# A hybrid SSD and GLA layer on one core: the order of the first block's start, and the step in which gates and the first y are made in blocks two to four

## The chip, the cores and the metric

The kernel runs on one core of one Trainium2 chip. The core has TensorE (PE, matmuls), VectorE (DVE), ScalarE (ACT), GpSimd (POOL) and SyncE (SP), which issues most transfers. The metric is the device time of one execution in microseconds, the median of three runs. Here it is 2259.13 us, with runs from 2258.09 to 2264.15.

## The reference

One decoder layer over 16 meta tokens and 2048 real tokens of width 1024, in float32. What is computed, cut to its core:

```python
u = rmsnorm(hres, norm_w)
proj = jnp.einsum('bld,dn->bln', u, w_in)          # one projection for all branches
z, xbc, dt_raw, q, k, v, g_gla, a_lr, merge_g = split_cols(proj, IN_WIDTHS)
# SSD branch: depthwise causal conv + silu on xbc, then a chunked scan with
# dt = softplus(dt_raw + dt_bias), decay exp(cumsum(dt * a)); y * silu(z), group rmsnorm
# GLA branch: log_a = log_sigmoid(a_lr @ gate_w2 + gate_b) / 16, chunked scan of q, k, v
# with cumsum(log_a); rmsnorm, * silu(g_gla)
branch_proj = jnp.einsum('blnc,ncd->blnd', branches, w_branch)
merged = jnp.sum(sigmoid(merge_g) * branch_proj, axis=2)
out = rmsnorm(hres + merged @ w_out, final_norm_w)[:, N_META:]
```

## The kernel before, in words

The 2048 tokens are cut into four blocks of 512 (the first also holds the 16 meta tokens). For each block all input projections but the merge gates are made, and the two scans are run; results go to DRAM. After the four blocks the merge gates, the two branch projections and the output projection follow as a chain of large matrix products, which the change does not touch.

**Matmuls in three parts.** Every operand is split into a rounded high part (ScalarE, Copy to fp32r) and a low remainder (a subtraction on VectorE for activations, on POOL for weights). `accum` (L207 to L211) issues three matmuls: high by high (L209), high by low (L210), low by high (L211). In block one the weights come raw from DRAM and are split by `load_w` (L163): the rounding is L171, the remainder L172. The split halves are stored (`save`, L201 to L205) and the later blocks read them back. There are 3 buffers for raw weights and 4 for split ones.

**The start.** `load_u` (L265) makes the normalised input u of a block. It squares and sums the rows, raises the mean to -1/2 on POOL (L279), spreads that over the partitions by matmuls with the identity (L317, L321), and then for each of eight tiles kt: load, normalise on VectorE (L333; in block one once for the 16 meta tokens and once for 512), round on ScalarE (L336), store, remainder on VectorE (L338). Behind it four small constants are halved on VectorE (L356 to L362).

**Pieces and steps.** In a block `enter` walks through a chain of pieces of TensorE work: generators such as `proj_zm` (the first z group, the step sizes dt and the gates' low-rank input), `proj_conv` (four tiles of one convolution group, one piece each), `proj_z` (block one) or `proj_z12` (other blocks), then the GLA projections. After each piece `step` advances every running generator by one part: `dt_chain`, `gates`, `ssd_scan`, `gla_scan`, `fetch_u`, `beside_unit`. Numbering pieces from n = 0, the pieces of a block are in sixes; with n = 6 * i the SSD scan of unit i - 1 begins.

- `gates` turns the low-rank input by TensorE (L460), evicts it, and for two pairs of heads multiplies by gw2 (L473), evicts it twice (L475 on VectorE, L476 on ScalarE), takes Exp (L478) and Ln (L479), then per head subtracts (L483) and runs sums along the chunks (L485). It begins at n = 6 in block one and at n = 8 in the others (L986).
- `ssd_scan` has a part for fetching, then `before(c)` and `after(c)` for four chunks: transposes (L637), their evictions (L640 to L646), the decay matrix on ScalarE (L650, L652) and its product with the scores on VectorE (L653); matmuls (L662, L663, L665), and their evictions (L668 to L675). A part scales by the root mean square (L703), and the last turns y by eight transposes (L708), evicts it on ScalarE (L710) and stores it (L711). The first unit begins at n = 6, so its y is turned at n = 13, the step of the last piece of `proj_z12`, whose banks are evicted by L494 and L495.

**What sets the order.** TensorE and SP issue in program order (a manual schedule, L1010). The order of VectorE, ScalarE and POOL is picked by a planner, which plays the program through with modelled times. `tc.issue_after(ins)` puts the instructions of a block behind `ins` on its engine; it adds an order, not a wait between engines. Banks of PSUM come from three pools: `pj` (3), `pt` (3) and `pc` (2).

Of the kernel before, what the change touches and what calls it, by code (L numbers as in the profile page):

```python
# [15 lines left out]
P = 128  # L16
# [21 lines left out]
T_SSD = 0  # L38
# [5 lines left out]
def trunk_kernel(ctx: ExitStack, tc: tile.TileContext, xm, xmt, w_feat, w_tok, w_v3, w_zm, w_br, w_o,  # L44
# [116 lines left out]
    kept, unsaved = {}, []  # L161

    def load_w(key, src):  # L163
        n = src.shape[-1]
        hl = mk(wpool, [P, 2, 512], F32R, "whl", bufs=4)[:, :, :n]
        if key in kept:
            nc.sync.dma_start(hl.bitcast(F32), kept[key])
        else:
            save(2)
            raw = raws.pop(key) if key in raws else load_raw(src)  # L170
            nc.scalar.activation(hl[:, 0], raw, AF.Copy)  # L171
            nc.gpsimd.tensor_tensor(hl[:, 1], raw, hl[:, 0].bitcast(F32), op=ALU.subtract)  # L172
# [20 lines left out]

    raws = {}

# [69 lines left out]
    def load_u(b):  # L265
# [10 lines left out]
        def rstd_rows(ss, n):  # L276
            r = mk(sm, [P, 1], F32, "rs1")
            nc.vector.tensor_scalar(r[:n], ss[:n], 1.0 / D, EPS, op0=ALU.mult, op1=ALU.add)
            nc.gpsimd.tensor_tensor(r[:n], r[:n], mhalf[:n, 0:1], op=ALU.pow)  # L279
            return r  # L280

# [27 lines left out]
        if m0:  # L309
            rs.append(rm_s)  # L310
            nc.sync.dma_start(cst[:, :2], cf32[:, :2])
# [12 lines left out]
        else:  # L324
            rbc = mk(spool, [P, 3 + META + BLK], F32, "cin")[:, :BLK]
            nc.scalar.activation(rbc, rb, AF.Copy)
            rbs = [(rbc, 0, BLK)]
            yield
        for kt in range(KT):
            xk = (mk(wk, [P, META + BLK], F32, "act", bufs=NACT) if m0 else mk(spool, [P, META + BLK], F32, "acc"))[:, :tt]  # L330
            nc.sync.dma_start(xk, xmt[:, kt, row0:row0 + tt])
            for ps, a, n in rbs:
                nc.vector.scalar_tensor_tensor(xk[:, a:a + n], xk[:, a:a + n], norm_w[:, kt:kt + 1], ps[:, :n],  # L333
                                               op0=ALU.mult, op1=ALU.mult)
            u.append(u_tile(b)[:, :, :tt])
            nc.scalar.activation(u[kt][:, 0], xk, AF.Copy)  # L336
            nc.scalar.dma_start(u_left[b][kt], xk[:, m0:])
            nc.vector.tensor_tensor(u[kt][:, 1], xk, u[kt][:, 0].bitcast(F32), op=ALU.subtract)  # L338
            yield
        return u  # L340

    next_u = {}

# [10 lines left out]

    hcw = const.tile([P, 16, 4], F32, name="hcw")
    nc.vector.tensor_scalar(hcw, conv_w, 0.5, None, op0=ALU.mult)  # L356
    hcb = const.tile([P, 16], F32, name="hcb")
# [3 lines left out]
    hgw = const.tile([P, 2], F32, name="hgw")  # L361
    nc.vector.tensor_scalar(hgw, gla_w, 0.5, None, op0=ALU.mult)  # L362
    nega = const.tile([P, NH], F32, name="nega")
    nc.scalar.activation(nega, hv[:, 1], AF.Exp)
# [39 lines left out]
    def dt_chain(o, psd):  # L404
# [12 lines left out]
        e = wde[:, :nck]  # L417
        nc.scalar.activation(e, x, AF.Abs)
        nc.scalar.activation(e, e, AF.Exp, scale=-1.0)
# [33 lines left out]
    def gates(o):  # L453
# [12 lines left out]
        for h2 in range(0, GH, 2):  # L466
# [14 lines left out]
            for h in (h2, h2 + 1):  # L481
                with tc.issue_after(convd[-1].ins) if m0 else nullcontext():
                    nc.vector.tensor_tensor(gmt[:, h % 2, :tt], gmt[:, h % 2, :tt], g_all[:, h, :tt], op=ALU.subtract)  # L483
                    for a, n in chunks:
                        nc.vector.tensor_tensor_scan(g_all[:, h, a:a + n], ones[:, :n], gmt[:, h % 2, a:a + n], 0.0,  # L485
                                                     op0=ALU.mult, op1=ALU.add)
                yield

# [11 lines left out]
    def proj_zm(o):  # L500
# [3 lines left out]
        yield from proj_tok("zm", w_zm, o.u, o.starts + [0] * o.ci0, list(enumerate(pss)), 288, 1, 256)  # L504
        begin(dt_chain(o, pss[NCH:] + pss[:NCH]))
        for c, ps in enumerate(pss[:NCH]):
            gate_z(zs[:, c], ps[:, :256])
        yield
# [82 lines left out]
    def ssd_scan(o, g):  # L591
# [37 lines left out]
        def before(c):  # L629
# [18 lines left out]
            with behind() if o.b == 0 else nullcontext():  # L648
# [3 lines left out]
                nc.scalar.activation(dm, dm, AF.Exp, scale=-1.0)  # L652
            nc.vector.tensor_tensor(dm, dm, scm[:, c].unsqueeze(1).to_broadcast([P, 4, P]), op=ALU.mult)  # L653
            held[c] = xdt, xw, bt, dm
# [47 lines left out]
        for c in range(NCH):  # L702
            nc.scalar.activation(yt[:, c], yt[:, c], AF.Identity, scale=r[:, c:c + 1])  # L703
        yield
        for j in range(2):
            ps = bank(pt, "pt")
# [246 lines left out]

    running, begun, lastly = [], [], []

    def begin(gen):
        begun.append(gen)

    def step():
        running.extend(begun)  # L960
        begun.clear()
        for gen in list(running) if len(running) < 2 or not lastly else list(running)[::-1]:
            if next(gen, running) is running:
                running.remove(gen)

    def beside_unit(key):
# [5 lines left out]
    def enter(pieces, o):  # L972
        b = o.b
        total = 6 * (SG + GH) + (b == nblk - 1)
        for n in range(total + 1):
            i, r = divmod(n, 6)
            if r == 0:
# [513 lines left out]
```

## Time and profile before

| | |
|---|---|
| median of 3 runs | 2259.13 us (2258.09 to 2264.15) |
| profiled execution | 2259.97 us, span 2257.6 us |
| mean granted TensorE clock | 0.996 |
| PE busy | 2217.3 us (98%) |
| DVE / ACT / POOL busy | 1575.8 / 1188.0 / 687.7 us |
| DRAM traffic | 517.94 MB in transfers, mean 229 GB/s |

A timeline row reads: start, duration in us, engine, source line, operation, output <- inputs, shapes, count; in square brackets the idle time before it and what ended that. A row of waits reads: engine, tile and line, what it waited for, us in total, times, the longest. A row of windows gives, for one stretch, the busy time of each engine with its instructions in brackets, then the granted TensorE clock (1.00 is full), the mean busy share of the 16 DMA engines, and GB/s. "x6" in a row means that six neighbours of one form were merged.

### The profile page before, as it was taken

The numbers are of one execution on the slowest core, as the hardware profiler recorded it, in microseconds if no ns is written. First come the engines' busy times: TensorE is split into PE (matmuls) and PEld (weight loads), VectorE is DVE, ScalarE is ACT, GpSimd is POOL, SyncE is SP. The second block draws the span as 40 slices with busy tenths as digits, with TensorE's granted clock in tenths as the row PEclk, the third lists the DMA queues.
The fourth block names the chain that finished last, engine by engine and source line by source line (L and its number), as shares of the span: only waits on it lengthen the run. The fifth ranks groups of instructions, "written<-read, shape, count | busy, mean of one in ns | idle before, by whom it ended". The sixth has DMA issues, their size and how long they took to land.

```text
span 2257.6 us, 34930 instructions
## 1 busy us (share of the span) xinstructions
PE 2217.3 (98%) x11789; PEld 1899.2 (84%) x11789; DVE 1575.8 (70%) x2935; ACT 1188.0 (53%) x2767; POOL 687.7 (30%) x681
## 2 busy tenths in 40 slices
PE   7999999999999999999999999999999999999998
PEld 6999989888888988888987888878888888888887
DVE  5776676677667676657677665684788855789966
ACT  4665655466445455544466454464644545554544
POOL 4344433222221122122122200066333264424341
PEclk9999999999999999999999999999999999999999
DMA  8666876667777666778666664376767866687753
GB/s 303 233 213 221 279 260 215 209 216 231 236 253 262 219 211 223 230 257 276 208 224 208 214 220 162 115 247 213 243 232 270 300 227 221 233 282 253 259 179 123
DMA packets 314210, 517.94 MB, mean 229 GB/s; under 512 B 28080, under 2 KB 162480, under 8 KB 314032
## 3 DMA queue, kind: packets, MB, share of 16 engines
q1 hardware_dynamic: 246864, 419.63, 56.6%
q10 hardware_dynamic: 67168, 96.10, 11.7%
q8 instruction: 92, 1.51, 0.3%
q14 instruction: 86, 0.70, 0.1%
HBM read 368.42 MB, written 147.19 MB: 228 GB/s over the span
## 4 chain that ended last, share of the span: by engine, by line
PE 88%; DVE 4%; ACT 3%; DMA 3%; issue 1%; POOL 1%; SPq 0%; ACTq 0%; POOLq 0%; DVEq 0%
PE pj L209 20%; PE pj L211 20%; PE pj L210 19%; PE pt L209 4%; PE pt L210 4%; PE pt L211 4%; PE pc L662 2%; PE pc L209 2%; PE pc L211 2%; PE pc L210 2%; PE pc L821 2%; PE pc L663 1%; PE pc L665 1%; PE pc L929 1%; DMA acc<-in_xmt 1%
## 5 line engine op out<-in xcount | busy, mean ns | idle before, releaser
L209 PE MATMUL pj<-ue,whl 128*128 128x264 f32 (+1 forms) x672 | 236.7, 352 | 3.9 <-ACT g_all L476 2.1
L211 PE MATMUL pj<-ue,whl 128*128 128x264 f32 (+1 forms) x672 | 231.1, 344 | 0.8 <-DVE tkc L421 0.8
L210 PE MATMUL pj<-ue,whl 128*128 128x264 f32 (+1 forms) x672 | 230.1, 342 | 0.0
L209 PE MATMUL pj<-uo,whl 128*128 128x512 f32 x512 | 205.7, 402 | 0.0
L211 PE MATMUL pj<-uo,whl 128*128 128x512 f32 x512 | 200.2, 391 | 0.0
L210 PE MATMUL pj<-uo,whl 128*128 128x512 f32 x512 | 199.4, 390 | 0.0
L209 PE MATMUL pj<-b,a 128*128 128x512 f32 (+1 forms) x484 | 188.7, 391 | 0.7 <-DVE io L1220 0.5
L210 PE MATMUL pj<-b,a 128*128 128x512 f32 (+1 forms) x484 | 187.7, 388 | 1.7 <-DVE b L1077 1.7
L211 PE MATMUL pj<-b,a 128*128 128x512 f32 (+1 forms) x484 | 188.9, 390 | 0.1
L573 DVE SCALAR_TENSOR_TENSOR acc<-cin,hcw,acc 128x512 f32<-128x512 f32 (+1 forms) x192 | 155.0, 807 | 42.2 <-ACT acc L569 41.1
L83 POOL TENSOR_TENSOR wr<-wr 128x256 f32<-128x256 f32 x80 | 66.9, 836 | 382.0 <-DMA wr<-u 159.1
L1102 DVE TENSOR_TENSOR a<-ar,a 128x512 fp32r<-128x512 f32 x160 | 132.8, 838 | 63.8 <-ACT a L1101 61.5
L1092 POOL TENSOR_TENSOR as<-ar,ar 128x512 f32<-128x512 f32 x40 | 62.1, 1553 | 376.9 <-DMA ar<-in_w_br 139.8
L209 PEld LDWEIGHTS pj<-ue,whl 128*128 128x128 f32 x672 | 127.7, 190 | 19.5 <-ACT g_all L476 2.3
L211 PEld LDWEIGHTS pj<-ue,whl 128*128 128x128 f32 x672 | 127.8, 190 | 15.9 <-POOL whl L172 1.0
L210 PEld LDWEIGHTS pj<-ue,whl 128*128 128x128 f32 x672 | 127.7, 190 | 14.8
L1077 DVE TENSOR_TENSOR b<-br,b 128x512 fp32r<-128x512 f32 x140 | 124.1, 909 | 22.3 <-ACT b L1076 21.7
L172 POOL TENSOR_TENSOR whl<-wr,whl 128x512 fp32r<-128x512 f32 (+1 forms) x76 | 97.1, 1286 | 134.4 <-ACT whl L171 95.1
L1102 DVE TENSOR_TENSOR a<-as,a 128x512 fp32r<-128x512 f32 x120 | 104.4, 871 | 44.3 <-ACT a L1101 42.0
L1136 ACT ACTIVATE sn<-pj 128x512 f32<-128x512 f32 x118 | 69.9, 593 | 118.5 <-PE pj L211 65.9
L1101 ACT ACTIVATE a<-ar 128x512 fp32r<-128x512 f32 x160 | 98.7, 624 | 55.8 <-PE pt L211 29.4
L1076 ACT ACTIVATE b<-br 128x512 fp32r<-128x512 f32 x140 | 85.9, 627 | 79.3 <-DMA br<-br_t 24.4
(328 smaller groups left out, 6500.2 us busy)
## 6 DMA issues: line engine op xcount, KB each, us to landing
whl<-k_s SPq DMA_DIRECT2D x96, 512.0 KB, 3.6
whl<-k_g SPq DMA_DIRECT2D x96, 512.0 KB, 4.1
whl<-k_v SPq DMA_DIRECT2D x36, 512.0 KB, 3.8
wr<-in_w_feat SPq DMA_DIRECT2D x64, 256.0 KB, 4.3
k_s<-whl SPq DMA_DIRECT2D x32, 512.0 KB, 3.7
cb<-cumd SPq DMA_DIRECT2D x64, 256.0 KB, 5.0
y<-gg ACTq DMA_DIRECT2D x64, 256.0 KB, 4.4
k_g<-whl SPq DMA_DIRECT2D x32, 512.0 KB, 3.8
```

Of the source, the lines that this page charges most:

```text
L83: nc.gpsimd.tensor_tensor(o, x, y, op=ALU.subtract)
L172: nc.gpsimd.tensor_tensor(hl[:, 1], raw, hl[:, 0].bitcast(F32), op=ALU.subtract)
L209: nc.tensor.matmul(ps, sh, mh, start=first, stop=False, **kw)
L210: nc.tensor.matmul(ps, sh, ml, start=False, stop=False, **kw)
L211: nc.tensor.matmul(ps, sl, mh, start=False, stop=last, **kw)
L573: convd[:] = [nc.vector.scalar_tensor_tensor(acc, cin[:, k:k + tt], hcw[:, ti, k:k + 1], acc, op0=ALU.mult, op1=ALU.add)]
L1076: nc.scalar.activation(t[:, 0], raw, AF.Copy)
L1077: nc.vector.tensor_tensor(t[:, 1], raw, t[:, 0].bitcast(F32), op=ALU.subtract)
L1092: nc.gpsimd.tensor_tensor(s1, a21, a22, op=ALU.add)
L1101: nc.scalar.activation(t[:, 0], src, AF.Copy)
L1102: latest[:] = [nc.vector.tensor_tensor(t[:, 1], src, t[:, 0].bitcast(F32), op=ALU.subtract)]
L1136: nc.scalar.activation(sn, self.ps[n, "a"], AF.Copy)
```

## The change

In block one:

- POOL's remainder of weight zm_0 (L172) is put behind the power of the last row chunk (L279).
- The normalising of tile kt (L333) is put behind the remainder (L338) of tile kt - 2.
- The four halved constants are put behind the remainder of the second tile.
- Both halves of the first convolution tile's weight, s0_0 and s0_1, are loaded and split at the end of `proj_zm`, ahead of the evictions; the z gate is put behind the first half's rounding, and the Abs of `dt_chain` (L418) behind the second's.
- The subtraction and sums of the gates (L483, L485) are issued at the end of a step, behind the last convolution step or the last product L653, whichever came later in the program.

In blocks two to four `gates` begins at n = 7 instead of 8, and `ssd_scan` of the first unit waits one step more before it turns y.

```diff
     def load_w(key, src):
+        if key in ready:
+            return ready.pop(key)
...
-            nc.scalar.activation(hl[:, 0], raw, AF.Copy)
-            nc.gpsimd.tensor_tensor(hl[:, 1], raw, hl[:, 0].bitcast(F32), op=ALU.subtract)
+            split_at[:] = [nc.scalar.activation(hl[:, 0], raw, AF.Copy)]
+            with tc.issue_after(first_rows[0].ins) if key == "zm_0" else nullcontext():
+                nc.gpsimd.tensor_tensor(hl[:, 1], raw, hl[:, 0].bitcast(F32), op=ALU.subtract)
...
+        lows = []
         for kt in range(KT):
...
-            for ps, a, n in rbs:
-                nc.vector.scalar_tensor_tensor(...)
+            with tc.issue_after(lows[kt - 2].ins) if m0 and kt > 1 else nullcontext():
+                for ps, a, n in rbs:
+                    nc.vector.scalar_tensor_tensor(...)
...
-            nc.vector.tensor_tensor(u[kt][:, 1], xk, u[kt][:, 0].bitcast(F32), op=ALU.subtract)
+            lows.append(nc.vector.tensor_tensor(u[kt][:, 1], xk, u[kt][:, 0].bitcast(F32), op=ALU.subtract))
+            if m0:
+                first_low[:] = lows[:2][-1:]
...
+    scaled_consts = tc.issue_after(first_low[0].ins)
+    scaled_consts.__enter__()
     nc.vector.tensor_scalar(hcw, conv_w, 0.5, None, op0=ALU.mult)
...
+    scaled_consts.__exit__(None, None, None)
...
-        nc.scalar.activation(e, x, AF.Abs)
+        with tc.issue_after(firsts[-1].ins) if m0 else nullcontext():
+            nc.scalar.activation(e, x, AF.Abs)
...
-                with tc.issue_after(convd[-1].ins) if m0 else nullcontext():
+                def sums(h=h):
                     nc.vector.tensor_tensor(gmt[:, h % 2, :tt], ...)
...
+                if m0:
+                    put_off.append(sums)
+                else:
+                    sums()
                 yield
...
-        begin(dt_chain(o, pss[NCH:] + pss[:NCH]))
-        for c, ps in enumerate(pss[:NCH]):
-            gate_z(zs[:, c], ps[:, :256])
+        if m0:
+            for i in range(2):
+                ready[f"s0_{i}"] = load_w(f"s0_{i}", w_feat[T_SSD, :, i * 512:(i + 1) * 512])
+                firsts.append(split_at[0])
+        with tc.issue_after(firsts[0].ins) if m0 else nullcontext():
+            begin(dt_chain(o, pss[NCH:] + pss[:NCH]))
+            for c, ps in enumerate(pss[:NCH]):
+                gate_z(zs[:, c], ps[:, :256])
...
-            nc.vector.tensor_tensor(dm, dm, scm[:, c].unsqueeze(1).to_broadcast([P, 4, P]), op=ALU.mult)
+            convd[:] = [nc.vector.tensor_tensor(dm, dm, scm[:, c].unsqueeze(1).to_broadcast([P, 4, P]), op=ALU.mult)]
...
             nc.scalar.activation(yt[:, c], yt[:, c], AF.Identity, scale=r[:, c:c + 1])
         yield
+        if not m0 and not g:
+            yield
         for j in range(2):
...
             if next(gen, running) is running:
                 running.remove(gen)
+        while put_off:
+            with tc.issue_after(convd[-1].ins):
+                put_off.pop()()
...
-            if b and n == 8:
+            if b and n == 7:
                 begin(gates(o))
```

More of the change, by code (lines that the diff above doesn't have):

```diff
@@ L161, in trunk_kernel @@
     kept, unsaved = {}, []
+    ready, split_at, firsts = {}, [], []
     def load_w(key, src):
+        if key in ready:
+            return ready.pop(key)
         n = src.shape[-1]
@@ L192, in load_half @@
         return hl[:, 0], hl[:, 1]
-    raws = {}
+    raws, first_rows = {}, []
     def load_raw(src):
@@ L278, in rstd_rows @@
             nc.vector.tensor_scalar(r[:n], ss[:n], 1.0 / D, EPS, op0=ALU.mult, op1=ALU.add)
-            nc.gpsimd.tensor_tensor(r[:n], r[:n], mhalf[:n, 0:1], op=ALU.pow)
-            return r
+            done = nc.gpsimd.tensor_tensor(r[:n], r[:n], mhalf[:n, 0:1], op=ALU.pow)
+            return (r, done) if m0 else r
         def rows_rstd(r0, n, vector):
@@ L310, in load_u @@
             rs.append(rm_s)
+            first_rows.append(rs[NCH - 1][1])
+            rs = [r for r, _ in rs]
             nc.sync.dma_start(cst[:, :2], cf32[:, :2])
@@ L331, in load_u @@
             nc.sync.dma_start(xk, xmt[:, kt, row0:row0 + tt])
-            for ps, a, n in rbs:
-                nc.vector.scalar_tensor_tensor(xk[:, a:a + n], xk[:, a:a + n], norm_w[:, kt:kt + 1], ps[:, :n],
-                                               op0=ALU.mult, op1=ALU.mult)
+            with tc.issue_after(lows[kt - 2].ins) if m0 and kt > 1 else nullcontext():
+                for ps, a, n in rbs:
+                    nc.vector.scalar_tensor_tensor(xk[:, a:a + n], xk[:, a:a + n], norm_w[:, kt:kt + 1], ps[:, :n],
+                                                   op0=ALU.mult, op1=ALU.mult)
             u.append(u_tile(b)[:, :, :tt])
@@ L337, in load_u @@
             nc.scalar.dma_start(u_left[b][kt], xk[:, m0:])
-            nc.vector.tensor_tensor(u[kt][:, 1], xk, u[kt][:, 0].bitcast(F32), op=ALU.subtract)
+            lows.append(nc.vector.tensor_tensor(u[kt][:, 1], xk, u[kt][:, 0].bitcast(F32), op=ALU.subtract))
+            if m0:
+                first_low[:] = lows[:2][-1:]
             yield
         return u
-    next_u = {}
+    first_low, next_u = [], {}
     def fetch_u(b):
@@ L951, in gla_scan @@
             nc.scalar.dma_start(y_left[1][o.b][2 * h + j], gs[j])
-    running, begun, lastly = [], [], []
+    running, begun, lastly, put_off = [], [], [], []
     def begin(gen):
```

## The prediction

> **What bounds the kernel now.** I read the page's busy times and its chain first, then the list of what TensorE waits for over the whole span, then the places of those waits in order of time.
>
> ```profile
> PE 2217.3 (98%) x11789; PEld 1899.2 (84%) x11789; DVE 1575.8 (70%) x2935; ACT 1188.0 (53%) x2767; POOL 687.7 (30%) x681
> ...
> PE 88%; DVE 4%; ACT 3%; DMA 3%; issue 1%; POOL 1%; SPq 0%; ACTq 0%; POOLq 0%; DVEq 0%
> ```
>
> TensorE is busy 2217.3 of 2257.6 us and carries 88% of the chain that ended last. The change adds no matmul, takes none away and resizes none. So it can only touch the 40 us in which TensorE is idle, and the stretches in which its clock is low. The waits (us in total, times, longest) that lie near the edited code:
>
> ```profile
> PE pt L637 <- ACT gg L710: 4.4, 3, 1.5
> PE pc L662 <- DVE sq L653: 3.6, 3, 3.2
> PE pj L209 <- ACT g_all L476: 2.1, 1, 2.1
> PE pj L209 <- ACT ue L336: 1.7, 2, 1.5
> PE pj L209 <- ACT whl L171: 1.6, 1, 1.6
> PE pj L211 <- DVE ue L338: 1.4, 1, 1.4
> PE pj L211 <- DVE tkc L421: 0.8, 1, 0.8
> ```
>
> The first is the one in blocks two to four, once in each. All the others are in block one (the 3.6 holds one of 3.2 there). Together they are 15.6 us, or 0.7% of the span; with what the clock loses after them this is the ceiling of the change. No row of this list points to anything in the products after the blocks, which the diff leaves alone.
>
> **Part 1, the start of block one (u's tiles and the first weights).** Rows in order of time, then the columns of a window: busy of PE, PEld, DVE, ACT, POOL, granted clock, DMA share, GB/s.
>
> ```profile
> 11.17 0.79 POOL L172 TENSOR_TENSOR whl<-wr,whl 128x288 fp32r<-128x288 f32 x1
> 11.92 0.54 POOL L279 TENSOR_TENSOR rs<-rs,mhalf 128x1 f32<-128x1 f32 x1
> 13.35 3.01 DVE L333 SCALAR_TENSOR_TENSOR act<-act,pv,pt 128x512 f32<-128x512 f32 x6 [0.52 <-PE pt L317]
> 16.28 0.70 DVE L338 TENSOR_TENSOR ue<-act,ue 128x528 fp32r<-128x528 f32 x1
> ...
> 18.61 0.61 PE L211 MATMUL pj<-whl,ue 128*128 128x288 f32 x1
> 31.61 0.80 POOL L172 TENSOR_TENSOR whl<-wr,whl 128x288 fp32r<-128x288 f32 x1 [2.67 <-DMA act<-in_gw]
> 24.00:27.00 3.00, 3.00 (x27) 3.00 (x25) 1.86 (x3) 0.16 (x1) 2.52 (x2) 1.00 1.01 367
> ```
>
> Two orders are turned round here. On POOL the split of weight zm_0 runs at 11.17 ahead of the last row's power at 11.92, and everything on VectorE waits for that power. With the new edge the power comes first: 11.92 - 11.17 = 0.75 us. On VectorE six normalising steps (3.01 us) run before the first remainder L338; the new edges let two tiles pass and then want that remainder, so about half of it, 1.5 us, goes. The second remainder follows one remainder of 0.70 later and no longer behind further pairs of tiles, for some 0.7 more. TensorE's unbroken run, from 18.61 today, begins 0.75 + 1.5 + 0.7, about 2.9 us, sooner. The four small scalings of constants that are moved behind the second remainder cost nothing while the first projection covers them: the convolution that reads them starts only after 36 us. Without that cover the next tile would wait less than one remainder, 0.70.
>
> How much of the 2.9 us lasts is set by the last weight of this projection, zm_7, split at 31.61 and used at once. Until 27 us the DMA engines are full (share 1.01 at 367 GB/s), so its bytes cannot come 2.9 us sooner if all that is queued ahead of them still moves. Bounds: 0 (transfers alone decide) to 2.9. I take 1.5, the middle, since the share of the window falls below full only after that.
>
> **Part 2, the end of block one's first projection.**
>
> ```profile
> 26.58 1.37 SPq L373 DMA_DIRECT2D act<-in_gw  x3
> 30.18 0.61 SPq L198 DMA_DIRECT2D wr<-in_w_feat  x1
> 36.89 0.63 ACT L171 ACTIVATE whl<-wr 128x512 fp32r<-128x512 f32 x1
> 37.58 0.39 PE L209 MATMUL pj<-ue,whl 128*128 128x264 f32 x1 [1.61 <-ACT whl L171]
> 38.92 0.59 PE L211 MATMUL pj<-ue,whl 128*128 128x264 f32 x1 [0.84 <-DVE tkc L421]
> 36.00:39.00 3.00, 0.59 (x3) 0.38 (x3) 1.84 (x6) 2.43 (x7) 1.27 (x1) 0.93 0.15 54
> 39.00:42.00 3.00, 3.00 (x14) 3.00 (x15) 1.90 (x4) 1.30 (x3) 2.14 (x2) 0.50 0.75 241
> ```
>
> The first convolution waits 1.61 us for ScalarE's rounding of its weight (36.89, behind the evictions) and 0.84 us for POOL's remainder of it, which the list books on L421. Then the granted clock is 0.50 for 3 us, a loss of 1.5 us. Together 3.95 us. The change issues both halves' loads, roundings and remainders before the evictions, and holds the z gate behind the first half, and the Abs of the step sizes' chain behind the second. What else moves: on SP's queue the two loads (and the stores that make room for them) pass the three loads of gw2 at 26.58 and the mask's. The mask is first read by the GLA scans, gw2 by the gates in step 7, both far later. The wait added on ScalarE has the z evictions queued behind it, and behind them TensorE's next banks; it costs nothing as long as the first half lands before TensorE ends the projection, near 35 us. Today's load is issued at 30.18, after gw2; without those it can go 2 to 3 us sooner. If it lands late, one eviction after another is late, at most the 1.61 us of today. Bounds 1.6 to 3.95, taken 3.4.
>
> [...]
>
> **Part 3, the running sums of the gates in block one.**
>
> ```profile
> 119.97 0.64 ACT L652 ACTIVATE sq<-sq 128x512 f32<-128x512 f32 x1
> 121.77 1.31 DVE L483 TENSOR_TENSOR tok<-tok,g_all 128x528 f32<-128x528 f32 x2
> 123.35 1.75 DVE L653 TENSOR_TENSOR sq<-sq,sq 128x512 f32<-128x512 f32 x1
> 125.15 1.97 PE L662 MATMUL pc<-c,sq 128*128 128x64 f32 x8 [3.16 <-DVE sq L653]
> 125.10:127.00 1.90, 1.85 (x9) 1.85 (x9) 1.90 (x3) 0.00 (x0) 1.12 (x1) 0.50 0.87 280
> 127.00:129.00 2.00, 2.00 (x7) 1.64 (x7) 2.00 (x7) 0.00 (x0) 0.81 (x1) 0.50 0.74 241
> 129.00:131.00 2.00, 2.00 (x12) 2.00 (x12) 1.97 (x7) 0.51 (x2) 0.00 (x0) 0.56 0.88 317
> ```
>
> L662 waits 3.16 us for the decay product L653. Its input was ready at 120.6 (119.97 + 0.64), but VectorE took two subtractions of the gates (L483) first. Put off behind that product, they start after it: L653 can run from 121.77 and, at the 0.7 us of its undisturbed runs rather than 1.75, end near 122.5; TensorE was ready at 125.15 - 3.16 = 122.0. So 0.5 us of wait is left and 2.6 go. The low clock after it costs 1.90 x 0.5 + 2 x 0.5 + 2 x 0.44 = 2.8 us. If it no longer falls, the part is worth 5.4 us; if VectorE is late anyway, nothing. I take 4.6. Next late are the sums themselves. Their readers are the scans of GLA, far behind. The wait of 2.1 us on L476 in step 10 stays: the same VectorE work stands ahead of it, in another order. Bounds for it -1 to +1, taken 0.
>
> **Part 4, blocks two to four.** First single rows, then windows of eight microseconds, about a step each, of block two.
>
> ```profile
> 487.24 0.41 DVE L673 TENSOR_TENSOR c<-c,pc 128x256 f32<-128x256 f32 x1
> 489.74 1.00 PE L662 MATMUL pc<-c,sq 128*128 128x64 f32 x8
> 513.26 1.28 ACT L710 ACTIVATE gg<-pt,hsw 128x512 f32<-128x512 f32 x2
> 514.02 0.55 PE L637 MATMUL pt<-cst,act 128*128 128x128 f32 x3 [1.50 <-ACT gg L710]
> 514.82 1.68 DVE L485 TENSOR_TENSOR_SCAN g_all<-ones_r,tok 128x128 f32<-128x128 f32 x5
> 478.00:486.00 8.00, 8.00 (x45) 6.47 (x44) 7.56 (x16) 4.79 (x13) 0.80 (x2) 1.00 0.57 199
> 486.00:494.00 8.00, 8.00 (x42) 6.82 (x41) 7.28 (x16) 5.67 (x10) 0.61 (x1) 1.00 0.48 162
> 494.00:502.00 8.00, 8.00 (x41) 6.66 (x40) 7.22 (x17) 3.13 (x9) 3.54 (x5) 1.00 0.74 233
> 502.00:510.00 8.00, 8.00 (x35) 6.11 (x34) 2.74 (x6) 6.04 (x11) 1.01 (x1) 1.00 0.70 229
> 510.00:518.00 8.00, 6.50 (x39) 5.50 (x38) 6.42 (x18) 7.83 (x20) 1.13 (x2) 1.00 0.79 268
> ```
>
> L637 wants a pt bank. The third is still z12's, and two hold the turned y, which ScalarE evicts at 513.26, being full (7.83 of 8 us) with the gates' second half and z12's evictions. The extra step takes the eight transposes L708, their two evictions and the two stores on ScalarE's queue out of that step and puts them behind the next convolution tile; the earlier chain moves the gates' second half to 494 to 502, where ScalarE has only 3.13 us of work. Both remove the wait: 4.4 us over three blocks. The clock is not part of it.
>
> Against that stands the first half, which moves from 486-494 to 478-486. ScalarE there has 4.79 us; with at most the 5.67 of the later window it is 10.5 in 8, a spill of 2.5 into a window that has just been emptied. VectorE has 7.56, and the sums of a head (four scans at 1.68 / 5, and a subtraction of 1.31 / 2: 2.0 us) come in at the next. L673, which frees the bank that L662 takes next, ends at 487.65, 2.1 us before 489.74. One head's sums ahead of it fit; two do not. Cost per block 0 to 2; I take 0.4, one block in five at its worst, 1.2 in all. The part is worth 3.2.
>
> **Sum.** 1.5 + 3.4 + 4.6 + 3.2 = 12.7 us off the profiled execution's 2259.97, whose span is 2257.6: 2247.3. The median of the three runs, 2259.13, is 0.84 below that execution, so 2246.4. Adding the ends of the four parts, the gains run from about 0 to 17 us; the likeliest case's own range is 2240 to 2252.
>
> **The rivals.** (a) *Block one gives nothing.* The full DMA holds zm_7 and the first convolution's halves, so the wait of part 2 only changes its name, and at 122 us the planner, which orders VectorE, ScalarE and POOL anew, puts other VectorE work ahead of L653. For it: share 1.01, and VectorE busy all through 125 to 129. Against: the edges name just those pairs. Left are 4.4 - 0.4: 2255. (b) *One of the two large parts of block one fails*, the other holds: 12.7 less 4.6, 8 us: 2251. (c) *Slower: VectorE in blocks two to four.* If both heads' sums come ahead of L673 (4.0 us against 2.1 of slack), L662 waits for its bank about 2, and 3 where POOL slows VectorE as L653 shows at 1.75, and the clock falls as at 125: 2.8. Three times (2.5 + 2.8) is 16, less 4.4 gained; with block one as in (a) that is 2259 + 11.5 = 2270.5, with block one at half its 9.5, 2266. It decides once more than 2.1 us of sums stand ahead of L673. For it: 7.56 and 7.28 of 8 us busy. Against: in program order the unit's own steps come before the gates'. (d) *The edits do not do what they say*, because the planner already finds these orders late: 2259.
>
> **Chances.** Forecast 0.50, (b) 0.18, (a) 0.14, (c) 0.10, (d) 0.08. A measurement of this kernel tells about 0.3%, 6.8 us, from no change: faster is below 2252.4, slower above 2265.9. Faster takes the forecast and most of (b): 0.64. Within takes (a), (d), the rest of (b), and the mild end of (c): 0.28. Slower 0.08. The range that leaves out 2 in 10, most of (c) above and the best ends below, is 2240 to 2260.
>
> **What would show it.** Right: no wait of L637 on L710 over 0.3 us; no wait of L662 on L653 over 1 us near 115 to 120; the first convolution's L209 starting before 35 us with the clock at 1.00; L710 at a place where ScalarE has room. Wrong: new waits of L662 or L665 on L673, or of z12 on L569, near 480 to 500 (c); L209 waiting for L171 after 34 us (a); VectorE's L483 still ahead of L653 (d).

## The result and the profile after

The changed kernel takes 2247.82 us, the median of 4 runs (2246.09 to 2248.57), and the kernel before took 2260.06 us, the median of 4 runs beside them. The ratio is 0.9938, with a 95% interval of 0.9927 to 0.9950. That is 14 us less by the ratio and 12.2 by the medians. The forecast was 2246.4 us, so it missed the median by 1.4 us. The profiled execution of the changed kernel took 2246.09 us with a span of 2244.0 us, 13.6 us less than the span before.

From the page of the changed kernel, the busy times and the shares of the chain that ended last:

```profile
PE 2213.1 (99%) x11789; PEld 1896.7 (85%) x11789; DVE 1574.2 (70%) x2935; ACT 1188.8 (53%) x2767; POOL 688.1 (31%) x681
...
PE 90%; DVE 3%; DMA 3%; ACT 2%; issue 1%; SPq 0%; POOL 0%; POOLq 0%; ACTq 0%; DVEq 0%
```

The same 11789 matmuls are busy for 4.2 us less than before (2217.3), and the idle time of TensorE falls from 40.3 us (2257.6 - 2217.3) to 30.9 (2244.0 - 2213.1), by 9.4. So about a third of the gain is busy time, in which the same matmuls took less, and two thirds are waits.

What TensorE still waits for in the changed kernel near the edits (engine, tile and line, what it waited for, us in total, times, the longest). The lines have moved: L209 to L211 are now L214 to L216, L336 to L338 are L345 to L347, L476 is L491, L653 is L678, L662 is L687, L637 is L662 and L710 is L737.

```profile
PE pj L214 <- ACT ue L345: 2.4, 2, 1.5
PE pj L214 <- ACT g_all L491: 2.2, 1, 2.2
...
PE pc L687 <- DVE sq L678: 0.8, 1, 0.8
...
PE pt L446 <- DVE ecu L443: 0.6, 1, 0.6
...
PE pc L646 <- DVE c L698: 0.3, 1, 0.3
```

Five of the seven rows shown of before are gone or small: the 4.4 us of blocks two to four, the waits of 1.6 and 0.8 at the first convolution and the 1.4 at the start have no row, and the 3.2 has become 0.8. The 2.1 us on the gates' eviction stands as it stood (2.2), and the wait for u's rounding has grown from 1.7 to 2.4. Small new ones are behind them (0.6 on L446, 0.3 on L646).

The timeline of the changed kernel, from the start to the first convolution:

```profile
14.37 0.61 PE L214 MATMUL pj<-whl,ue 128*128 128x288 f32 x1 [1.51 <-ACT ue L345]
15.45 0.35 ACTq L346 DMA_DIRECT2D u<-act  x1
15.90 0.64 ACT L345 ACTIVATE ue<-act 128x528 fp32r<-128x528 f32 x1 [1.58 <-DVE act L342]
16.60 0.61 PE L214 MATMUL pj<-whl,ue 128*128 128x288 f32 x1 [0.86 <-ACT ue L345]
...
29.39 0.81 POOL L177 TENSOR_TENSOR whl<-wr,whl 128x288 fp32r<-128x288 f32 x1 [0.99 <-ACT whl L175]
...
34.46 0.37 PE L214 MATMUL pj<-ue,whl 128*128 128x264 f32 x1
...
35.31 0.39 PE L214 MATMUL pj<-ue,whl 128*128 128x264 f32 x1 [0.24 <-ACT alr L428]
```

The first convolution begins at 34.46, before 37.58, and waits 0.24 us where it waited 1.61 and 0.84. The last weight of the projection, zm_7, is split at 29.39, before at 31.61. That difference is not the change's: the five experiments below that have the old start split it at 28.83, 29.11, 29.88, 29.23 and 29.57, so 31.61 was late in that one execution. The start itself is less good than the edges promise: the second tile's rounding (15.90) stands behind the issue of the first tile's store (15.45) on ScalarE, and TensorE waits 0.86 us for it.

Windows of the changed kernel (busy of PE, PEld, DVE, ACT, POOL, then granted clock, DMA share, GB/s):

```profile
36.00:39.00 3.00, 3.00 (x27) 3.00 (x26) 1.30 (x4) 0.96 (x4) 0.28 (x1) 1.00 1.04 410
39.00:42.00 3.00, 2.40 (x19) 2.15 (x18) 1.80 (x5) 2.97 (x7) 1.62 (x2) 1.00 0.92 358
...
105.00:107.00 2.00, 2.00 (x11) 2.00 (x11) 2.00 (x6) 2.00 (x7) 0.00 (x0) 0.50 0.08 23
...
119.00:121.00 2.00, 2.00 (x14) 1.90 (x15) 2.00 (x2) 0.77 (x2) 1.68 (x2) 1.00 1.05 298
121.00:123.00 2.00, 2.00 (x19) 2.00 (x18) 2.00 (x3) 0.27 (x1) 2.00 (x2) 1.00 0.84 286
```

The clock no longer falls behind the first convolution, nor behind the decay product near 119 us. It still falls to 0.50 behind the wait of 2.2 us that stayed, near 105.

### The profile page after: what moved, and what is told of

Same layout as the page of the kernel before. It is cut to its first block, busy times and chain, and to the rows that moved or that the text cites. A ratio compares the mean times of both kernels' runs of the same rounds, so it can differ in the third digit from the quotient of the medians.

```text
span 2244.0 us, 34943 instructions
## 1 busy us (share of the span) xinstructions
PE 2213.1 (99%) x11789; PEld 1896.7 (85%) x11789; DVE 1574.2 (70%) x2935; ACT 1188.8 (53%) x2767; POOL 688.1 (31%) x681
## 4 chain that ended last, share of the span: by engine, by line
PE 90%; DVE 3%; DMA 3%; ACT 2%; issue 1%; SPq 0%; POOL 0%; POOLq 0%; ACTq 0%; DVEq 0%
PE pj L214 20%; PE pj L216 20%; PE pj L215 20%; PE pt L214 4%; PE pt L215 4%; PE pt L216 4%; PE pc L687 2%; PE pc L214 2%; PE pc L216 2%; PE pc L215 2%; PE pc L848 2%; PE pc L688 1%; PE pc L690 1%; PE pc L956 1%; PE pt L662 1%
## 5 line engine op out<-in xcount | busy, mean ns | idle before, releaser
L214 PE MATMUL pj<-ue,whl 128*128 128x264 f32 (+1 forms) x672 | 236.3, 352 | 3.1 <-ACT g_all L491 2.2
L216 PE MATMUL pj<-ue,whl 128*128 128x264 f32 (+1 forms) x672 | 230.4, 343 | 0.0
L214 PE MATMUL pj<-uo,whl 128*128 128x512 f32 x512 | 205.7, 402 | 0.0
L216 PE MATMUL pj<-uo,whl 128*128 128x512 f32 x512 | 200.1, 391 | 0.0
L214 PE MATMUL pj<-b,a 128*128 128x512 f32 (+1 forms) x484 | 188.7, 391 | 0.7 <-DVE io L1250 0.5
L216 PE MATMUL pj<-b,a 128*128 128x512 f32 (+1 forms) x484 | 188.9, 390 | 0.0
L598 DVE SCALAR_TENSOR_TENSOR acc<-cin,hcw,acc 128x512 f32<-128x512 f32 (+1 forms) x192 | 155.5, 810 | 41.6 <-ACT acc L594 40.3
L1107 DVE TENSOR_TENSOR b<-br,b 128x512 fp32r<-128x512 f32 x140 | 128.7, 941 | 23.3 <-ACT b L1106 22.4
L214 PEld LDWEIGHTS pj<-ue,whl 128*128 128x128 f32 x672 | 127.0, 189 | 19.4 <-ACT g_all L491 2.4
L216 PEld LDWEIGHTS pj<-ue,whl 128*128 128x128 f32 x672 | 127.1, 189 | 14.9
L215 PE MATMUL pt<-b,a 128*128 128x512 f32 x320 | 125.4, 392 | 0.1
```

The source lines that it names most:

```text
L214: nc.tensor.matmul(ps, sh, mh, start=first, stop=False, **kw)
L215: nc.tensor.matmul(ps, sh, ml, start=False, stop=False, **kw)
L216: nc.tensor.matmul(ps, sl, mh, start=False, stop=last, **kw)
L598: convd[:] = [nc.vector.scalar_tensor_tensor(acc, cin[:, k:k + tt], hcw[:, ti, k:k + 1], acc, op0=ALU.mult, op1=ALU.add)]
L1107: nc.vector.tensor_tensor(t[:, 1], raw, t[:, 0].bitcast(F32), op=ALU.subtract)
```

## Where the time went, place by place

TensorE's instructions are issued in program order (the manual schedule of L1010), so the same matmul can be found in every trace. The scores of the first SSD unit, first in the kernel before and then in the changed one:

```profile
78.79 1.06 PE L621 MATMUL pc<-act,act 128*128 128x128 f32 x8
```

```profile
74.81 1.06 PE L646 MATMUL pc<-act,act 128*128 128x128 f32 x8
```

At this place the changed kernel is 3.98 us early. The table gives this difference in us at five places, named by their time in the kernel before: the running sums of the step sizes, between the first and the second convolution tile (45.99), the first unit's scores (78.79), later scores in block one (181.60), the first scores of block two (465.43), and the last of block four (1302.12). The kernels in the lower rows are those of the experiments below.

| kernel | 45.99 | 78.79 | 181.60 | 465.43 | 1302.12 |
|---|---|---|---|---|---|
| changed | 4.33 | 3.98 | 7.72 | 7.13 | 13.74 |
| start alone | 1.77 | 1.90 | 1.67 | 1.33 | 1.27 |
| convolution's weights alone | 4.06 | 3.41 | 2.96 | 2.80 | 3.31 |
| put-off sums alone | 1.67 | 1.82 | 5.63 | 5.62 | 5.01 |
| blocks two to four alone | -0.95 | -0.68 | 0.14 | 0.06 | 6.20 |
| gates earlier alone | 0.81 | 1.08 | 1.99 | 1.62 | 5.89 |
| y turned later alone | 1.03 | 1.30 | 2.09 | 1.89 | 2.68 |
| changed, later stores | 6.99 | 6.36 | 7.58 | 7.44 | 12.60 |
| changed, later sums | 5.61 | 4.97 | 12.18 | 11.98 | 18.75 |
| changed, later sums, again | 4.54 | 3.90 | 10.51 | 10.24 | 17.16 |
| changed, both later | 6.16 | 5.52 | 11.08 | 10.89 | 17.74 |
| changed, both later, again | 6.69 | 6.05 | 10.92 | 10.74 | 16.91 |

The four kernels in the middle that leave the start alone (put-off sums, blocks two to four, gates, y) stand at 1.67, -0.95, 0.81 and 1.03 at 45.99. They run the same program up to there. So one execution's start is known to no better than 1 or 2 us, and a step is read from the difference of two columns rather than from one. Two causes are in the traces: the end of a slow phase at the start, told of in the last section, and the late zm_7 of the kernel before, by which it loses 1.15 us between 31.2 and 32.7 us to every other trace. A fairer zero is therefore the mean of those four, 0.64 at 45.99 and 0.88 at 78.79: the changed kernel is 3.7 and 3.1 us ahead of it.

## The experiments

### Each part alone

**The start alone** (the edges on the power, the normalising order and the four constants; nothing else).

```diff
+            with tc.issue_after(first_rows[0].ins) if key == "zm_0" else nullcontext():
+                nc.gpsimd.tensor_tensor(hl[:, 1], raw, hl[:, 0].bitcast(F32), op=ALU.subtract)
...
+            with tc.issue_after(lows[kt - 2].ins) if m0 and kt > 1 else nullcontext():
+                for ps, a, n in rbs:
```

> The kernel before with the edits of the start of block one alone (power before the first weight's remainder, normalising two tiles behind the remainders, constants behind them). Theory: the first tiles come about 1.3 us sooner but TensorE stays at half rate longer and the first convolution still waits for its weight, so the second convolution tile starts 0.5 to 1 us sooner, and the time is 2259 (no more than 1 us gained). Rival (the prediction's size): the start keeps 1.5 us or more, to 2.9, the time is 2256.5 to 2258.

Measured: ratio 0.9995 (0.9985 to 1.0004), which cannot be told from no change. The trace gives 1.3 to 1.9 us over the kernel before, within the spread of the starts.

**The first convolution's weights alone** (both halves loaded and split ahead of the evictions).

```diff
+        if m0:
+            for i in range(2):
+                ready[f"s0_{i}"] = load_w(f"s0_{i}", w_feat[T_SSD, :, i * 512:(i + 1) * 512])
+                firsts.append(split_at[0])
+        with tc.issue_after(firsts[0].ins) if m0 else nullcontext():
+            begin(dt_chain(o, pss[NCH:] + pss[:NCH]))
```

> The kernel before with the first convolution's weight halves loaded and split ahead of the evictions, alone. Theory: this holds most of the 4.0 us that block one's start gave in the whole change: 3 to 3.6 us (both waits of 1.61 and 0.84 gone, the clock at 1.00 through 36 to 42), time 2256 to 2257. Rival: it needs the faster start, because the first half's load lands too late without it; then under 2 us, and TensorE's first matmul of the convolution still waits for L171.

Measured: ratio 0.9983 (0.9974 to 0.9993), 3.8 us by its middle. From its timeline (its L213 is L209):

```profile
36.36 0.39 PE L213 MATMUL pj<-ue,whl 128*128 128x264 f32 x1 [0.97 <-ACT alr L418]
...
50.33 0.39 PE L213 MATMUL pj<-ue,whl 128*128 128x264 f32 x1 [0.69 <-ACT acc L579]
```

The waits of 1.61 and 0.84 on the weight are gone. Waits of 0.97 and 0.69 on evictions have come in their place. 4.06 us at 45.99 become 2.8 to 3.4 later.

**The put-off sums alone.**

```diff
-                with tc.issue_after(convd[-1].ins) if m0 else nullcontext():
+                def sums(h=h):
...
+        while put_off:
+            with tc.issue_after(convd[-1].ins):
+                put_off.pop()()
```

> The kernel before with the gates' sums of block one put off behind the decay product, alone. Theory: 3.7 us, as between 4.0 and 7.7 in the whole change: the wait of 3.16 falls to about 0.8, the clock stays up there; the wait of 2.1 on the gates' eviction stays at 2.1. Time 2255.5 to 2256.5. Rival: the wait only moves to another product or bank in the same two steps, under 1.5 us are gained.

Measured: ratio 0.9985 (0.9976 to 0.9995), 3.4 us. From its timeline (L667 is L662 before):

```profile
105.24 0.39 PE L209 MATMUL pj<-ue,whl 128*128 128x264 f32 x1 [2.12 <-ACT g_all L476]
...
121.08 1.10 PE L667 MATMUL pc<-c,sq 128*128 128x64 f32 x8 [0.80 <-DVE sq L658]
```

The wait of 3.16 is 0.80, the one of 2.1 stands. Between 78.79 and 181.60 the table gains 3.81 for this kernel and 3.74 for the changed one.

**Blocks two to four alone** (gates at n = 7 and y turned a step later).

```diff
+        if not m0 and not g:
+            yield
...
-            if b and n == 8:
+            if b and n == 7:
```

> The kernel before with the two edits of blocks two to four alone. Theory: 2.2 us per block, 6.7 in all, time 2252.5 to 2253.5: the wait of 1.5 per block cost more than its idle time, and the earlier chain costs nothing. Rival (the prediction's size): 3.2 us in all, the rest of what the whole change gained there belonging to block one's edits; time 2256.

Measured: ratio 0.9965 (0.9952 to 0.9978), 7.9 us, and 6.14 us in the trace from 465.43 to 1302.12 (6.61 in the changed kernel). The middles of the four single ratios add to 1.1 + 3.8 + 3.4 + 7.9 = 16 us, the whole gave 14, with an interval of 11 to 16.5. So the parts add up as far as this measurement can tell.

### The two edits of blocks two to four apart

```diff
-            if b and n == 8:
+            if b and n == 7:
```

> The kernel before with the gates' chain one piece sooner in blocks two to four, y turned where it was. Theory: ScalarE is free of the second half when z12 and y are evicted, so the wait of L637 falls from 1.5 to under 0.5 and most of the 2.2 us per block are gained, 4 to 6.7 in all; time 2253 to 2256. Rival (c of the prediction): the chain's first half overloads VectorE and ScalarE in steps 8 and 9, and new waits of L662, L665 or a bank of 0.5 us and more appear there; time 2257 or above.

```diff
+        if not m0 and not g:
+            yield
         for j in range(2):
```

> The kernel before with the first unit's y turned a step later in blocks two to four, the gates where they were. Theory: the two pt banks of the turned y are what L637 lacked, so its wait goes, though ScalarE is still full there; 4 to 6 us in all, time 2253 to 2256. Rival: ScalarE's second half of the gates delays z12's evictions all the same, L637 or the next convolution's pj bank waits 1 us or more, and under 2 us are gained.

Measured: the gates alone 0.9973 (0.9963 to 0.9983), the y alone 1.0000 (0.9991 to 1.0009). First the row of the gates alone, then that of the y alone:

```profile
511.10 0.55 PE L637 MATMUL pt<-cst,act 128*128 128x128 f32 x3 [0.34 <-ACT gg L710]
```

```profile
517.53 0.63 PE L710 MATMUL pt<-cst,tok 128*128 128x128 f32 x4 [1.61 <-DVE tok L495]
```

With the gates earlier, the wait of L637 falls from 1.50 to 0.34. With y turned later and the gates where they were, L637 no longer waits, and the transposes themselves wait 1.61 us for the banks of z12. There the wait has only moved. So what came late was the evictions of that step, on ScalarE and VectorE, and turning y later pays only for what the earlier gates have left: some 0.5 us in the stretch shown next (89.36 against 88.81). The ratios of the gates alone (0.9973) and of both edits (0.9965) do not tell the two apart.

What the wait costs is read from one stretch, from the scores at 465.43 to those at 556.62, in windows of before, of the changed kernel, of the gates alone and of the y alone:

```profile
465.43:556.62 91.19, 89.48 (x458) 74.68 (x457) 70.42 (x144) 57.99 (x145) 23.47 (x35) 1.00 0.68 219
```

```profile
458.30:547.11 88.81, 88.81 (x459) 74.85 (x458) 70.07 (x144) 57.95 (x145) 23.66 (x35) 1.00 0.71 225
```

```profile
463.81:553.17 89.36, 89.02 (x459) 74.83 (x458) 68.92 (x144) 58.01 (x145) 23.08 (x35) 1.00 0.72 223
```

```profile
463.54:554.25 90.71, 89.10 (x459) 74.75 (x458) 69.43 (x144) 57.67 (x145) 24.38 (x35) 1.00 0.70 220
```

Before, TensorE was idle 91.19 - 89.48 = 1.71 us in it: the 1.50 of L637, and 0.21 that L662 waited 6.6 us later:

```profile
520.60 1.10 PE L662 MATMUL pc<-c,sq 128*128 128x64 f32 x8 [0.21 <-DVE sq L653]
```

After, it is never idle. But the stretch is 2.38 us shorter, so 0.67 us is booked as busy time, at a granted clock of 1.00 in both. The two waits thus cost 1.4 times what their rows say (2.38 / 1.71). Other executions repeat it: with the old order of these blocks (the start, the weights and the sums alone) the stretch took 91.44, 90.89 and 90.88 us with 1.78, 1.50 and 1.50 idle, and with blocks two to four alone it took 88.80 with none. Part of the rest is the matmul before a wait: a row of eight scores lasts 1.06 us with starts 0.11 apart, so the last one is booked with some 0.27, of which a next matmul covers all but 0.11 where there is no wait. Where the whole 0.67 lies is not shown. The same work of ScalarE is done in the same stretch (57.99 and 57.95), only elsewhere in it. The five windows of the prediction from 478 to 518 lie 7.13 us earlier in the changed kernel:

```profile
470.87:478.87 8.00, 8.00 (x46) 6.94 (x45) 8.00 (x16) 7.47 (x14) 0.80 (x2) 1.00 0.59 196
478.87:486.87 8.00, 8.00 (x42) 6.81 (x41) 8.00 (x21) 3.32 (x10) 1.05 (x1) 1.00 0.52 172
486.87:494.87 8.00, 8.00 (x39) 6.34 (x38) 5.90 (x12) 2.14 (x6) 3.67 (x5) 1.00 0.71 226
494.87:502.87 8.00, 8.00 (x37) 6.60 (x36) 4.47 (x13) 7.87 (x17) 1.01 (x1) 1.00 0.72 228
502.87:510.87 8.00, 8.00 (x46) 6.92 (x45) 5.43 (x13) 7.11 (x23) 1.80 (x2) 1.00 0.84 268
```

Against before, ScalarE has more work in the first and the fourth of them (7.47 for 4.79, 7.87 for 6.04) and less in the other three, 7.11 for 7.83 in the last among them, where L637 had waited. VectorE is full in the first two (8.00 of 8 us), and no row of L687 or L690 waits for it there.

### The store in ScalarE's queue at the start

The second tile's rounding stood behind a DMA issue. This kernel is the changed one with block one's stores of u issued two tiles later.

```diff
-            nc.scalar.dma_start(u_left[b][kt], xk[:, m0:])
+            held.append((u_left[b][kt], xk[:, m0:]))
+            with tc.issue_after(high.ins):
+                while len(held) > (2 if m0 and kt < KT - 1 else 0):
+                    nc.scalar.dma_start(*held.pop(0))
```

> The changed kernel with block one's stores of u issued two tiles later on ScalarE's queue. In the changed kernel's trace the rounding of the second tile waits behind the store of the first, which ScalarE issues at 15.45 only, 1.1 us after the first rounding ended. Theory: this queue, not VectorE's order, holds the second tile; the second rounding starts near 14.5 instead of 15.9, TensorE's unbroken run 1.2 us sooner, and 0.5 to 1.5 us are kept; time 2246.5 to 2247.5. Rival: the half clock and the full DMA take it all, nothing is kept, 2247.8 or more.

Measured: 2246.74 us, ratio 0.9937 (0.9920 to 0.9953), the same as the changed kernel. From its timeline:

```profile
14.60 0.65 ACT L345 ACTIVATE ue<-act 128x528 fp32r<-128x528 f32 x1 [0.16 <-DVE act L342]
...
17.04 0.35 ACTq L349 DMA_DIRECT2D u<-act  x1
...
75.44 0.55 PE L665 MATMUL pt<-cst,act 128*128 128x128 f32 x3 [1.95 <-ACT g_all L494]
...
118.53 1.57 PE L690 MATMUL pc<-c,sq 128*128 128x64 f32 x8 [1.98 <-DVE sq L681]
```

The store was what held the rounding: it now runs at 14.60 instead of 15.90, and the place at 45.99 is reached 2.7 us sooner than in the changed kernel. (About half of that, by an estimate from the spacings of the matmuls in the last section, is the slow phase of the start, which ended at 20.02 us in this execution and at 22.63 in that of the changed kernel.) By 181.60 nothing of it is left, since two waits of 1.95 and 1.98 have come in, one on the gates' eviction and one on the decay product. TensorE arrives sooner; ScalarE and VectorE, which are what it waits for, do not.

### The wait that stayed, near 103 us

In the changed kernel VectorE takes the sums of the second head ahead of the next pair's evictions, which hold the banks. Its rows, then those of a kernel in which these sums come behind the evictions (its L491 is L490, its L692 is L687), and a window of the latter:

```profile
97.86 3.98 DVE L500 TENSOR_TENSOR_SCAN g_all<-ones_r,tok 128x16 f32<-128x16 f32 x5
...
102.08 0.48 DVE L490 TENSOR_SCALAR tok<-pj,pv 128x264 f32<-128x264 f32 x1
...
103.13 0.39 PE L214 MATMUL pj<-ue,whl 128*128 128x264 f32 x1 [2.16 <-ACT g_all L491]
```

```profile
98.01 0.48 DVE L491 TENSOR_SCALAR tok<-pj,pv 128x264 f32<-128x264 f32 x1
...
106.76 1.10 PE L692 MATMUL pc<-c,sq 128*128 128x64 f32 x8 [0.66 <-DVE sq L683]
```

```profile
105.00:107.00 2.00, 1.34 (x12) 1.10 (x11) 2.00 (x5) 1.98 (x3) 0.57 (x1) 1.00 0.74 226
```

```diff
+            if carry:
+                put_off.append((carry.pop(), low))
...
-                if m0:
-                    put_off.append(sums)
+                if m0 and h == 1:
+                    carry.append(sums)
+                elif m0:
+                    put_off.append((sums, None))
...
-            with tc.issue_after(convd[-1].ins):
-                put_off.pop()()
+            fn, anchor = put_off.pop()
+            with tc.issue_after((anchor or convd[-1]).ins):
+                fn()
```

> The changed kernel with the sums of head 1 in block one put behind the next pair's evictions on VectorE. The wait of 2.16 us on the gates' eviction is still there after the change. Theory: VectorE's sums ahead of L475 are its cause; the wait falls to under 0.5, the clock does not fall after it, 3.5 to 4.2 us are gained; time 2243.5 to 2244.5. Rival: VectorE is full there whatever its order, the wait moves to the next decay product or to the second pair's banks; under 1.5 us.

Measured: 2241.98 us, ratio 0.9920 (0.9905 to 0.9935). The evictions run 4.07 us sooner (98.01 against 102.08; about 1 us of it is this execution's earlier start), the wait of 2.16 is gone, the clock stays at 1.00, and a wait of 0.66 comes in. From 78.79 to 181.60 this kernel gains 7.21 us (6.61 in its second execution below), the changed one 3.74, so the order of these sums is worth 2.9 to 3.5 us.

### Both later edits

Put together, once with rounds of its own and once beside the later sums on one chip.

> The changed kernel with both later edits: block one's u stores issued two tiles later, and the put-off sums of the first head pair taken up behind the next pair's evictions on L490. Theory 1, each wait of block one costs on its own: the run with the later sums alone stood at 2242.0 us, and the start that the later stores bring was 2.7 us earlier at the second convolution tile, of which 2.0 us were lost again in a wait near 75 us and 2.0 us in one near 118 us; the second of these is the wait that the later sums remove, so 2239.5 to 2241 us is expected, with the wait near 75 us still in the records. Theory 2, what the start gains is taken back before 181 us whatever follows, since VectorE and ScalarE are late and not TensorE: 2241.5 to 2243 us, no difference from the later sums alone.

> The changed kernel with the later sums, timed once more so that it stands beside the kernel with both edits on one chip: 0.9915 to 0.9925 of the kernel before, by both theories.

> The later sums and the later stores together, beside the later sums alone on the same chip. Theory 1, the stores' start is kept once the wait near 118 us is gone: 1 to 2.5 us less than the later sums alone, 0.9905 to 0.9915. Theory 2, the start is taken back in a wait near 75 us whatever follows: within 0.7 us of the later sums alone, so 0.9915 to 0.9925.

Measured: both 2240.57 us, ratio 0.9897 (0.9879 to 0.9915). Side by side: the later sums 2243.45 us (2242.67 to 2246.28), ratio 0.9921 (0.9906 to 0.9936); both 2240.87 us (2238.68 to 2242.36), ratio 0.9904 (0.9888 to 0.9921). The medians differ by 2.6 us and the runs do not overlap, as theory 1 has it, though the intervals of the ratios do. The places in the traces speak for theory 2: at 45.99 both stand 2.15 us ahead of the later sums alone, at 181.60 only 0.41, at 1302.12 behind them by 0.25. The first row is of the later sums, the second of both:

```profile
77.13 0.55 PE L667 MATMUL pt<-cst,act 128*128 128x128 f32 x3 [1.18 <-ACT g_all L492]
```

```profile
75.52 0.88 PE L670 MATMUL pt<-cst,act 128*128 128x128 f32 x3 [1.73 <-ACT g_all L495]
```

The execution that was profiled is the slowest of its four for both kernels with both edits (2243.65 and 2242.36), so the traces may not show what the others gain. In the second (mean granted clock 0.998), the clock fell to 0.50 for 3.41 us behind the wait of 1.73 (from 75.58; the 264-wide matmuls start 0.22 us apart from 76.42 to 78.84 and 0.12 to 0.13 after 79.04), at a cost of up to 1.7 us, an estimate from half of 3.41; in the first (0.999) it did not fall behind a wait of 1.93 at the same place. So the places speak for theory 2 only weakly, and where the 2.6 us lie stays open. Either version came out faster than the changed kernel both times; with both edits the kernel runs about 1% faster than before.

## Why the prediction was right, point by point

The forecast time was right within 1.4 us, and the mechanism of parts 2 to 4 held in the main, but the closeness is in part luck: one term was 3.4 us too small, and misses of 0.9, 0.9 and 0.6 us the other way made up for most of it.

- **Parts 1 and 2, 1.5 + 3.4 = 4.9.** Measured together 4.33 us at 45.99 and 3.98 at 78.79; against the mean of the four old starts 3.7 and 3.1. The weights' term held (2.8 to 4.1 alone), with the clock at 1.00 from 36 to 42 us. Of the start, the three terms 0.75 + 1.5 + 0.7 were read as one gain of 2.9 at TensorE. Its unbroken run began 1.26 us sooner (16.60, before 17.86; the 18.61 of the prediction is a matmul inside that run). The power's edge brought 0.45 (the first 512-wide normalising at 12.90, before 13.35), the order of the remainders the 1.5 (first remainder at 14.36, before 16.28), and the 0.7 became a loss of 0.66 (second remainder at 16.58, before 17.84), because "the second remainder follows one remainder of 0.70 later" overlooked the store in ScalarE's own queue, ahead of the rounding that the remainder needs. Whether the full DMA (share 1.04 from 24 to 27 us in the changed kernel) holds back zm_7's bytes, as the bound of 0 had it, is open: the row at 31.61 on which this rested was one late execution, old and new starts both split zm_7 near 29, and in no trace but that one does TensorE wait for it. Alone the start could not be told from no change, so 1.5 for it is not contradicted and not shown.
- **Part 3, 4.6.** Measured 3.7 at 181.60 (3.8 alone). The steps held nearly to the tenth: the decay product takes 0.68 and not 1.75, the wait left is 0.77 against 0.5 expected, the clock stays at 1.00, and the wait on L476 stays (2.16). Some 0.5 us went to two small waits behind it, of 0.31 on L646 and 0.23 on L214.
- **Part 4, 3.2.** Measured 6.6 us, twice as much: this is the term that was mis-sized. Two steps failed. "Cost per block 0 to 2; I take 0.4" charged 1.2 us for VectorE's load; VectorE did become full (8.00 of 8 us in two windows), but no matmul waited for it. And 4.4 counted the idle time of the wait alone, after "it can only touch the 40 us in which TensorE is idle, and the stretches in which its clock is low", while the stretches around the three waits became 2.38, 2.17 and 2.49 us shorter at a granted clock of 1.00. Also, "Both remove the wait" is true of the gates but for 0.34; the y alone moves it.
- **The rest, 13.6 against 12.7.** From 181.60 to 465.43 the changed kernel loses 0.6 us, a loss which no step of the sum named; it is small beside the spread of these traces.
- **The rivals.** (a) and (b) fall, since each large part gave its gain alone. (c) falls: VectorE is full from 470.87 to 486.87, and neither L662's nor L665's successor waits there. (d) falls with the single ratios of three of the four parts. The time of (a) is off by its own terms: "4.4 - 0.4" takes the cost of one block, where the sum takes 1.2 for three, so it would be 2256.

## What to carry to other kernels

A wait can be worth more than its row (here 2.38 us where the rows say 1.71): add the smaller waits that follow it and what is booked as busy around it, from two windows over the same work. When an engine's order is moved ahead, look for what stands ahead in the order of the engine between, transfers' issues among it (here a store's issue at 15.45 ahead of the rounding at 15.90). And an earlier arrival is kept only if the engines that free the banks are early too; the start stood 2.7 us further ahead with later stores and had lost it by 181.60, while taking the sums from in front of the evictions lasted to the end.

## What the runs showed of the hardware

**The start has a slow phase that the clock column does not show.** Windows of one microsecond of the kernel before:

```profile
21.00:22.00 1.00, 1.00 (x7) 1.00 (x7) 1.00 (x3) 0.70 (x3) 0.07 (x1) 1.00 1.06 390
22.00:23.00 1.00, 1.00 (x11) 1.00 (x10) 1.00 (x2) 1.00 (x3) 0.75 (x1) 1.00 1.05 404
```

The same 288-wide matmuls start 0.24 us apart at first and 0.13 later (before: 20.21, 20.45 and 20.69, then 23.59, 23.72 and 23.86), with a granted clock of 1.00 in every row. The trace's records of the clock begin with a rise to 1.00, at 21.53 us in the kernel before, at 22.63 in the changed kernel, and at 20.10 with the same start alone; ahead of the first record the column shows 1.00 for want of one. So the changed kernel started its unbroken run 1.26 us sooner, but its rise came 1.10 us later, and at the matmul that ran at 23.11 before, 0.19 us was left. The point of the rise varies: with later stores it lies at 20.02. In these four executions (before, changed, start alone, later stores) the first matmul of the projection starts at 14.83, 14.37, 14.21 and 14.49 us, so the rise comes 6.70, 8.26, 5.89 and 5.53 us behind it. What sets it is not shown.

**Gaps of like length, with a fall of the clock and without.** In the kernel before the granted clock is 0.50 from 38.59 to 42.01, from 106.86 to 110.28 and from 123.93 to 130.76 us, and in the changed kernel from 104.55 to 107.96: 3.41 us each, but 6.83 the third. These falls begin 17.07, 85.33 and 102.40 us behind the rise at 21.53, and 81.92 behind the one at 22.63, which is 5, 25, 30 and 24 times 3.41. Windows of 3.41 us, of the changed kernel and then of the one with later stores:

```profile
101.14:104.55 3.41, 1.42 (x11) 1.43 (x12) 3.41 (x9) 1.96 (x6) 0.41 (x1) 1.00 0.52 150
104.55:107.96 3.41, 3.41 (x18) 3.41 (x17) 3.41 (x9) 3.39 (x10) 0.00 (x0) 0.50 0.23 67
```

```profile
98.53:101.94 3.41, 2.07 (x15) 1.75 (x13) 3.41 (x8) 0.17 (x1) 2.19 (x3) 1.00 0.75 215
101.94:105.35 3.41, 2.63 (x21) 2.63 (x22) 3.41 (x10) 3.16 (x11) 0.00 (x0) 1.00 0.05 16
115.60:119.01 3.41, 1.43 (x12) 1.22 (x12) 3.41 (x6) 2.14 (x7) 1.38 (x2) 1.00 0.27 90
119.01:122.42 3.41, 3.41 (x14) 3.05 (x14) 3.41 (x4) 0.47 (x2) 3.41 (x3) 0.50 0.93 279
```

In these executions the length of a gap did not decide alone. In the changed kernel the first window holds 1.99 us of the gap of 2.16, and the clock falls at its end. With later stores a gap of 2.12 at the same place is cut at 101.94, which is 24 times 3.41 behind the rise of that execution, into 1.34 and 0.78, and the clock stays at 1.00, while the gap of 1.98 before 118.53 lies in one window, and it falls. In the kernel before, the windows of 3.41 us ahead of its three falls hold 2.12, 1.92 and 1.94 us of idle time. That the idle time within such a window decides is the author's reading of these few gaps. The gaps of 1.50 us in blocks two to four left the clock at 1.00 (with 0.67 us more booked as busy).
